# Two networks in one kernel on one core: the modulation's sums on VectorE are tied to the weight chunks, and spread at other rates

## The chip, the cores and the metric

One core of one Trainium2 chip runs one program. The metric is the device time of an execution in microseconds (us); a smaller one is better.

## What is computed

A block of a first network, with a state-space branch, a gated delta rule, a convolved gated feed-forward layer and norms, feeds a block of a second one. All tensors are float32, with 256 tokens and 2048 features. What the change touches is the second block's modulation: one vector `c` times a wide matrix, whose six parts shift, scale and gate what is around them.

```python
mod = jax.nn.silu(c) @ ada_w + ada_b
mod_c = jax.nn.silu(c_ctx) @ ada_w + ada_b
sh1, sc1, g1, sh2, sc2, g2 = jnp.split(mod[:, None, :], 6, axis=-1)
...
z = modulate(rmsnorm_2(x, norm1_g), sh1, sc1) @ w_in
zc = modulate(rmsnorm_2(xc, norm1_g), sh1c, sc1c) @ w_in
...
x = x + g1 * (jnp.concatenate([attn, rw], axis=-1) @ w_out)
x = x + g2 * swiglu(modulate(rmsnorm_2(x, norm2_g), sh2, sc2), ffn_w1, ffn_w3, ffn_w2)
```

Here `x` is the output of the first block, and `xc` is a context of 256 tokens that depends on no first block. So the columns of the context (`zc @ w_in`, and the recurrence over it) can run beside the first block's feed-forward layer.

## The kernel before

**Dense products.** Every large product is a call of `dense`. It walks through its weights in chunks of 128 x 2 x 512 floats (512 KB). `wchunk` loads a chunk into a tile `w` (three buffers, issued on SP's queue), ScalarE rounds it to a tile `wr` (L268, two buffers), and VectorE subtracts the rounded part from the chunk and leaves the rest in `wl` (L269, two buffers). TensorE then runs 24 matmuls of 256 columns on a full chunk: 16 with `wr` (L297 and L298), 8 with `wl` (L300), into accumulators `acc`, of which there are three. After the last chunk of a product ScalarE and VectorE empty the accumulators.

**The modulation.** Its first third (`ada_cols`) is a chain of matmuls and ends near 690 us. The rest is done by VectorE in `ada_rows`: a tile `w_ada` of 128 x 512 floats (256 KB) of the transposed matrix is loaded (L183, SP's queue, three buffers, two loads ahead), and one instruction (L241, called a sum below) multiplies it with a broadcast row of `c` (`ada_c`) and adds up along the row. There are 192 sums for columns 32 to 79 of `mod` and 64 for columns 80 to 95. `ada_rows` is a generator; `dense` adds `tick_rate` per chunk and runs one step of it for each whole tick, so that the rate says how many sums are traced for each chunk.

**The order.** The program is traced as the code is written, and a scheduler that goes by priorities and a simulated timeline then writes the order of each engine's queue. Each engine runs its queue in that order. The sums stand in a block of lowered priority (`high_priority(offset=-300)`): the scheduler puts them wherever it believes VectorE to have nothing better to do.

**The program's stages**, with the times at which they run in the profile of before: the last product of the first block's mixer (`w_out1`), the norm of the context, its columns (`ctx_path`) and the first slices of the feed-forward layer with the context's first recurrences, 840 to 1290 us; three more of these recurrences (`ctx_quads`) among slices of the feed-forward layer, 1290 to 1560 us; the feed-forward layer alone (`ffn1`), 1560 to 2040 us; the norms between the blocks and the columns of `x` (`rw_x`, `attn_cols`), 2040 to 2350 us; mostly attention, 2350 to 2580 us; the last recurrences, the output norms `rw_out`, the products `w_out2` and a norm, 2580 to 2780 us; the last feed-forward layer (`ffn2`), 2780 to 3520 us. Results of the 192 sums are first used after attention (`w_out2`), those of the 64 in the last products of `ffn2`.

Of the kernel before, what the change touches and what calls it, by code (L numbers as in the profile page):

```python
# [10 lines left out]
F32 = mybir.dt.float32  # L11
# [3 lines left out]
ALU = mybir.AluOpType  # L15
# [74 lines left out]
class Kern:  # L90
# [130 lines left out]
    def ada_rows(self, n0, n1):  # L221

        nc = self.nc
        W = self.a["ada_wT"].rearrange("(n p) k -> p n k", p=128)
        steps = [(q, n) for q in range(4) for n in range(n0, n1)]
        load = lambda q, n: self.ada_tile(W[:, n - 32, q * 512:q * 512 + 512])

        ahead = [load(*st) for st in steps[:2]]
        for i, (q, n) in enumerate(steps):
            if n == n0:  # L230
                ps = self.ps.tile([128, 512], F32, tag="ada", name="ada_c", bufs=1)
                for j in range(4):
                    k = q * 4 + j
                    nc.tensor.matmul(ps[:, j * 128:j * 128 + 128], lhsT=self.sil[:, k:k + 1].to_broadcast([128, 128]),
                                     rhs=self.C("ident"), start=j == 0, stop=j == 3)
            if i + 2 < len(steps):
                ahead.append(load(*steps[i + 2]))
            w = ahead.pop(0)

            with self.tc.high_priority(offset=-300):  # L240
                nc.vector.scalar_tensor_tensor(w, w, 1.0, ps, ALU.mult, ALU.mult,  # L241
                                               accum_out=self.part[:, n - n0, q:q + 1])
            yield n
        m = self.mod[:, 0, n0:n1]
        nc.vector.reduce_sum(m, self.part[:, :n1 - n0], axis=mybir.AxisListType.X)
        nc.vector.tensor_tensor(m, m, self.P("ada_b")[:, n0:n1], ALU.add)
# [15 lines left out]
    def wchunk(self, src, kb, w):  # L262
        nc = self.nc
        t = self.pw.tile([128, 2, 512], F32, tag="w", name="w", bufs=self.NW)
        nc.sync.dma_start(t[:, :kb, :w], src)
        r = self.pw.tile([128, 2, 512], F32R, tag="wr", name="wr", bufs=self.NWR)
        l = self.pw.tile([128, 2, 512], F32R, tag="wl", name="wl", bufs=self.NWL)
        nc.scalar.copy(r[:, :kb, :w], t[:, :kb, :w])  # L268
        nc.vector.tensor_tensor(l[:, :kb, :w], t[:, :kb, :w], r[:, :kb, :w].bitcast(F32), ALU.subtract)  # L269
        return r, l  # L270

    def dense(self, W, KT, c0, w, xh, xl, evac, r0=0):
# [1511 lines left out]
    def program(self, out):  # L1784
        self.setup()
        self.norm1()
        self.ada_start()
        self.qkv()
        self.deltanet()
        self.z_gate()  # L1790
        self.u_proj()
        self.dn_out()
        self.s5_setup()
        self.s5()
        self.dn_proj()
        self.gs_gate()
        self.s5_out()
        self.glu()
        self.w_out1()
        self.ada_next()  # L1800
        self.tick_rate = 0.54
        self.mod1()
        self.rw_setup()
        self.ctx_path()
        self.ffn1_norm()
        self.ctx_quads()
        self.ffn1()
        self.mid_norms()
        self.rw_x(0)
        self.run(self.rw_xq(0))  # L1810
        self.rw_x(1)
        self.attn_cols()
        self.ada_end()
        self.attention()
        self.early([self.rw_xq(1, ()), self.rw_xq(2, ('AR',)), self.rw_xq(3, ('AR',))])
        self.attn_split()
        self.x3_load()
        self.w_out2(0)
        self.rw_out_gate()
        for hq in range(4):  # L1820
            self.rw_out(hq)
        self.w_out2(1)
        self.ada_last()
        self.ffn2()
        self.final(out)
# [105 lines left out]
```

## Time and profile before

| | |
|---|---|
| median of three runs | 3553.86 us (3543.9 to 3554.04) |
| the profiled execution, its own time | 3542.68 us |
| its span, first to last instruction | 3540.7 us |
| TensorE busy | 3367.7 us (95%) |
| VectorE busy | 2431.7 us (69%) |
| ScalarE busy | 1511.8 us (43%) |
| bytes moved by DMA | 601.60 MB, mean 170 GB/s |
| mean granted TensorE clock | 0.974 |

Busy time of an engine is the time in which at least one of its instructions ran. TensorE's matmuls overlap and their ends are modelled, so that a busy TensorE is not always at its best rate. The granted clock is the share of TensorE's full clock that the chip let through, 1.00 or 0.50 at any moment. What lies outside the span is 2 us.

### The profile page before, as it was taken

To read this page: it belongs to the slowest core of one execution; us is meant where nothing else is said; L and a number is where in the kernel's file an instruction comes from. 1 tells how busy PE (TensorE), PEld (TensorE's weight loads), DVE (VectorE), ACT (ScalarE), POOL (GpSimd) and SP (SyncE) were. 2 spreads that over 40 slices of the span, in tenths; PEclk is the share of its full clock that TensorE was granted. 3 is DMA by queue.
4 is the path that set the end of the run, shared out by engine and by line. 5 is a ranking of instruction groups with operands and counts; after the bars stand their busy time and mean duration, and the time that the engine had idled before them with its cause. 6 is when DMAs were issued, how large, how long until landed. Compare 5 with 4: busy or idle time off the path is not lost. (4 is left out here: it accounts for less than half of the span.)

```text
span 3540.7 us, 72779 instructions
## 1 busy us (share of the span) xinstructions
PE 3367.7 (95%) x30748; PEld 3076.5 (87%) x30748; DVE 2431.7 (69%) x3987; ACT 1511.8 (43%) x2147; POOL 17.1 (0%) x46
## 2 busy tenths in 40 slices
PE   8999999999998899999999998997898999999998
PEld 6779877898988789899999988885686999999998
DVE  5676787867779778866665677586668655555556
ACT  4434433444344444444444454444433443433433
POOL 0000000000000000000000000000000000000000
PEclk9999999999998999999999999998899999999999
DMA  6644555557887543345555554350045555555554
GB/s 222 195 149 138 171 172 194 169 180 265 285 277 232 182 158 125 124 138 179 178 181 183 175 155 127 115 153 3 33 144 199 167 183 184 183 184 182 182 185 149
DMA packets 328071, 601.60 MB, mean 170 GB/s; under 512 B 24160, under 2 KB 48480, under 8 KB 327744
## 3 DMA queue, kind: packets, MB, share of 16 engines
q1 hardware_dynamic: 327520, 595.88, 52.2%
q8 instruction: 241, 3.95, 0.4%
q0 software_dynamic: 224, 1.07, 0.1%
q14 instruction: 86, 0.70, 0.1%
HBM read 591.61 MB, written 4.72 MB: 168 GB/s over the span
## 5 line engine op out<-in xcount | busy, mean ns | idle before, releaser
L269 DVE TENSOR_TENSOR wl<-w,wr 128x1024 fp32r<-128x1024 f32 (+2 forms) x928 | 1109.3, 1197 | 718.0 <-ACT wr L268 669.9
L268 ACT CAST wr<-w 128x1024 fp32r<-128x1024 f32 (+2 forms) x928 | 953.1, 1028 | 1416.2 <-PE acc L298 1153.1
L297 PE MATMUL acc<-hh,wr 128*128 128x256 f32 (+2 forms) x4976 | 1256.9, 288 | 29.2 <-ACT hh L1053 5.4
L298 PE MATMUL acc<-hl,wr 128*128 128x256 f32 (+2 forms) x4976 | 1248.1, 286 | 1.1 <-DVE hl L316 0.6
L297 PEld LDWEIGHTS acc<-hh,wr 128*128 128x128 f32 (+2 forms) x4976 | 958.9, 193 | 74.2 <-issue 24.8
L298 PEld LDWEIGHTS acc<-hl,wr 128*128 128x128 f32 (+2 forms) x4976 | 960.0, 193 | 14.7 <-issue 11.7
L300 PE MATMUL acc<-hh,wl 128*128 128x256 f32 (+2 forms) x4976 | 754.7, 288 | 24.1 <-DVE wl L269 23.7
L300 PEld LDWEIGHTS acc<-hh,wl 128*128 128x128 f32 (+2 forms) x4976 | 661.7, 193 | 69.9 <-DVE wl L269 35.9
L297 PE MATMUL acc<-hid,wr 128*128 128x256 f32 x1408 | 355.2, 286 | 3.7 <-DVE x L1127 3.4
L298 PE MATMUL acc<-hid,wr 128*128 128x256 f32 x1408 | 353.6, 284 | 0.0
L297 PEld LDWEIGHTS acc<-hid,wr 128*128 128x128 f32 x1408 | 271.1, 193 | 7.7 <-DVE x L1127 4.1
L298 PEld LDWEIGHTS acc<-hid,wr 128*128 128x128 f32 x1408 | 271.3, 193 | 0.9 <-issue 0.7
L300 PE MATMUL acc<-hid,wl 128*128 128x256 f32 x1408 | 224.8, 286 | 0.8 <-DVE wl L269 0.8
L241 DVE SCALAR_TENSOR_TENSOR w_ada<-w_ada,ada_c 128x512 f32<-128x512 f32 x256 | 170.1, 681 | 61.6 <-DMA w_ada<-in_ada_wT_dram 58.8
L300 PEld LDWEIGHTS acc<-hid,wl 128*128 128x128 f32 x1408 | 192.5, 192 | 4.0 <-issue 2.1
L1106 DVE SCALAR_TENSOR_TENSOR fconv<-acc,pv,fconv 128x255 f32<-128x255 f32 (+1 forms) x176 | 81.3, 477 | 23.1 <-ACT fconv L1104 21.5
L200 PE MATMUL ada_ps<-w_ada,pv 128*32 128x512 f32 x256 | 84.6, 604 | 4.4 <-DMA w_ada<-in_ada_w_dram 4.4
L1104 ACT ACTIVATE fconv<-acc,pv 128x256 f32<-128x256 f32 x88 | 40.4, 471 | 60.2 <-DVE fconv L1106 32.8
L1351 PE MATMUL rw_ps<-rw_AR,rw_BK 64*128 64x64 f32 (+1 forms) x512 | 62.4, 294 | 3.8 <-ACT rw_BKT L1358 3.6
L297 PE MATMUL acc<-mrgh,wr 128*128 128x256 f32 x256 | 63.7, 286 | 1.6 <-DVE x L1034 0.9
L1351 PEld LDWEIGHTS rw_ps<-rw_AR,rw_BK 64*128 64x128 f32 x512 | 53.8, 198 | 11.7 <-ACT rw_BKT L1358 3.8
L298 PE MATMUL acc<-ys5l,wr 128*128 128x256 f32 x256 | 63.6, 283 | 0.0
(538 smaller groups left out, 3727.0 us busy)
## 6 DMA issues: line engine op xcount, KB each, us to landing
w<-in_w_dram SPq DMA_DIRECT2D x264, 512.0 KB, 3.6
w<-in_w_in_dram SPq DMA_DIRECT2D x256, 512.0 KB, 3.9
w<-in_ffn_up_dram SPq DMA_DIRECT2D x176, 512.0 KB, 3.7
w_ada<-in_ada_wT_dram SPq DMA_DIRECT2D x256, 256.0 KB, 4.0
w<-in_ffn_down_dram SPq DMA_DIRECT2D x88, 512.0 KB, 3.6
w_ada<-in_ada_w_dram SPq DMA_DIRECT2D x128, 256.0 KB, 3.4
w<-in_w_out_dram SPq DMA_DIRECT2D x64, 512.0 KB, 4.6
w<-in_glu_w_dram SPq DMA_DIRECT2D x32, 512.0 KB, 3.6
```

The costliest lines, as they stand in the source:

```text
L200: nc.tensor.matmul(ps[32 * g:32 * g + 32, :], lhsT=self.pv[:, o + kt:o + kt + 32], rhs=ahead.pop(0), start=kt == 0, stop=kt == 15)
L241: nc.vector.scalar_tensor_tensor(w, w, 1.0, ps, ALU.mult, ALU.mult, accum_out=self.part[:, n - n0, q:q + 1])
L268: nc.scalar.copy(r[:, :kb, :w], t[:, :kb, :w])
L269: nc.vector.tensor_tensor(l[:, :kb, :w], t[:, :kb, :w], r[:, :kb, :w].bitcast(F32), ALU.subtract)
L297: nc.tensor.matmul(o, lhsT=a, rhs=xh(kt), start=kt == 0 and first_j, stop=False)
L298: nc.tensor.matmul(o, lhsT=a, rhs=xl(kt), start=False, stop=False)
L300: nc.tensor.matmul(o, lhsT=a, rhs=xh(kt), start=False, stop=kt == KT - 1 and last_j)
L1104: nc.scalar.activation(t[:, j], ps[:, j], AF.Copy, scale=w(2))
L1106: v.scalar_tensor_tensor(t[:, j, k:], ps[:, j, :256 - k], w(2 - k), t[:, j, k:], ALU.mult, ALU.add)
L1351: nc.tensor.matmul(pss[e][:, c], lhsT=bk(d, c)[hs[e]], rhs=AR[hs[e], d, :, cs], start=True, stop=True)
```

## The change

`wchunk` keeps the subtraction that it traced last as `self.wsub`. Each sum is traced in a block that puts it behind that subtraction in VectorE's queue; no wait on a semaphore is added. The rate, 0.54 sums for each chunk from `mod1` to `attn_cols` before, is 0.2 up to `ffn1_norm`, 0.55 through `ctx_quads` and `ffn1`, and 0.43 after that. `ffn2` keeps its 0.5.

```diff
-            with self.tc.high_priority(offset=-300):
+            with self.tc.high_priority(offset=-300), self.tc.issue_after(self.wsub.ins):
                 nc.vector.scalar_tensor_tensor(w, w, 1.0, ps, ALU.mult, ALU.mult,
                                                accum_out=self.part[:, n - n0, q:q + 1])
...
         nc.scalar.copy(r[:, :kb, :w], t[:, :kb, :w])
-        nc.vector.tensor_tensor(l[:, :kb, :w], t[:, :kb, :w], r[:, :kb, :w].bitcast(F32), ALU.subtract)
+        self.wsub = nc.vector.tensor_tensor(l[:, :kb, :w], t[:, :kb, :w], r[:, :kb, :w].bitcast(F32), ALU.subtract)
...
         self.ada_next()
-        self.tick_rate = 0.54
+        self.tick_rate = 0.2
         self.mod1()
         self.rw_setup()
         self.ctx_path()
         self.ffn1_norm()
+        self.tick_rate = 0.55
         self.ctx_quads()
         self.ffn1()
+        self.tick_rate = 0.43
         self.mid_norms()
```

The scheduler writes other orders from this. The first place is VectorE's queue at the end of an early slice of the first feed-forward layer, near 1190 us in the profile of before. `fconv` is the convolved output of a slice, `invDT` belongs to the recurrence over the context. Before:

```order
L241 SCALAR_TENSOR_TENSOR w_ada,part<-w_ada,ada_c 128x512 x2
L1119 TENSOR_TENSOR fconv<-fconv 128x512
L241 SCALAR_TENSOR_TENSOR w_ada,part<-w_ada,ada_c 128x512 x6
L269 TENSOR_TENSOR wl<-w,wr 128x1024
L241 SCALAR_TENSOR_TENSOR w_ada,part<-w_ada,ada_c 128x512 x2
L636 SCALAR_TENSOR_TENSOR invDT<-inv_11663,cst,invDT 128x16x16
```

And now:

```order
L1106 SCALAR_TENSOR_TENSOR fconv<-acc_13913,pv,fconv 128x254
L1119 TENSOR_TENSOR fconv<-fconv 128x512
L269 TENSOR_TENSOR wl<-w,wr 128x1024
L636 SCALAR_TENSOR_TENSOR invDT<-inv_11615,cst,invDT 128x16x16
L269 TENSOR_TENSOR wl<-w,wr 128x1024
L241 SCALAR_TENSOR_TENSOR w_ada,part<-w_ada,ada_c 128x512
L637 STREAM_TRANSPOSE invD<-invDT 128x512
```

Eight sums stood just ahead of one subtraction and two behind it; now none stands ahead of it, and a single one behind the next.

The second place is VectorE's queue in `rw_out`, near 2690 us. `xr` is an output of the recurrence, `rw_nsq` its norm. Before:

```order
L1565 SCALAR_TENSOR_TENSOR xr_25136<-rw_mean,xr_25136 128x256 x2
L241 SCALAR_TENSOR_TENSOR w_ada,part<-w_ada,ada_c 128x512 x2
L1565 SCALAR_TENSOR_TENSOR xr_25136<-rw_mean,xr_25136 128x256
L241 SCALAR_TENSOR_TENSOR w_ada,part<-w_ada,ada_c 128x512
L416 RECIPROCAL rw_nsq<-rw_nsq 64x256
L241 SCALAR_TENSOR_TENSOR w_ada,part<-w_ada,ada_c 128x512
L416 RECIPROCAL rw_nsq<-rw_nsq 64x256
L241 SCALAR_TENSOR_TENSOR w_ada,part<-w_ada,ada_c 128x512 x2
L1575 SCALAR_TENSOR_TENSOR xr_25136<-xr_25136,pv,rw_rs 128x256 x2
```

And now:

```order
L1565 SCALAR_TENSOR_TENSOR xr_25085<-rw_mean,xr_25085 128x256 x2
L416 RECIPROCAL rw_nsq<-rw_nsq 64x256 x2
L1575 SCALAR_TENSOR_TENSOR xr_25085<-xr_25085,pv,rw_rs 128x256 x2
L1576 SCALAR_TENSOR_TENSOR xr_25085<-xr_25085,pv,xv_24818 128x256 x2
L1577 TENSOR_TENSOR xr_25085<-xr_25085,rw_G_29704 128x256 x2
L316 TENSOR_TENSOR rwl_29732<-xr_25085,rwh_29730 128x256 x2
```

All 64 sums of the last part stood in this stretch; it now has four, none of them between these steps.

The third place is VectorE's queue in `ffn1` alone, near 1665 us. `hid` is the hidden layer's rounded rest. Before:

```order
L269 TENSOR_TENSOR wl<-w,wr 128x1024
L1106 SCALAR_TENSOR_TENSOR fconv<-acc_18076,pv,fconv 128x255
L1106 SCALAR_TENSOR_TENSOR fconv<-acc_18075,pv,fconv 128x255
L1106 SCALAR_TENSOR_TENSOR fconv<-acc_18076,pv,fconv 128x254
L1106 SCALAR_TENSOR_TENSOR fconv<-acc_18075,pv,fconv 128x254
```

And now:

```order
L269 TENSOR_TENSOR wl<-w,wr 128x1024
L241 SCALAR_TENSOR_TENSOR w_ada,part<-w_ada,ada_c 128x512
L1106 SCALAR_TENSOR_TENSOR fconv<-acc_18031,pv,fconv 128x255
L1106 SCALAR_TENSOR_TENSOR fconv<-acc_18030,pv,fconv 128x255
L1106 SCALAR_TENSOR_TENSOR fconv<-acc_18031,pv,fconv 128x254
L1106 SCALAR_TENSOR_TENSOR fconv<-acc_18030,pv,fconv 128x254
```

A sum now stands behind about every second subtraction of the layer, here ahead of four instructions that empty accumulators; before, the layer alone had none.

By the chunk behind which they stand, with the times that the chunks have in the profile of before, the 256 sums lie as follows:

| stretch, us | sums before | sums now |
|---|---|---|
| to 840 | 6 | 0 |
| 840 to 1290 | 186 | 32 |
| 1290 to 1560 | 0 | 34 |
| 1560 to 2040 | 0 | 88 |
| 2040 to 2350 | 0 | 36 |
| 2350 to 2580 | 0 | 2 |
| 2580 to 2780 | 64 | 4 |
| 2780 to 3520 | 0 | 60 |

The loads of `w_ada` move on SP's queue with the sums: before, up to 15 of them follow each other there; now each stands alone among the loads of `w`. TensorE's and ScalarE's queues hold the same work with small shifts of place.

## Rows read from the trace of the kernel before

**Rows 1.** The page: busy time of the engines; then the two VectorE groups.

```profile
PE 3367.7 (95%) x30748; PEld 3076.5 (87%) x30748; DVE 2431.7 (69%) x3987; ACT 1511.8 (43%) x2147; POOL 17.1 (0%) x46
...
L269 DVE TENSOR_TENSOR wl<-w,wr 128x1024 fp32r<-128x1024 f32 (+2 forms) x928 | 1109.3, 1197 | 718.0 <-ACT wr L268 669.9
...
L241 DVE SCALAR_TENSOR_TENSOR w_ada<-w_ada,ada_c 128x512 f32<-128x512 f32 x256 | 170.1, 681 | 61.6 <-DMA w_ada<-in_ada_wT_dram 58.8
```

**Rows 2.** Span and mean granted clock of the core.

```profile
core 0: 3540.7 us, clock 0.974
```

**Rows 3.** Busy time by stretch, granted clock, DMA share and rate.

```profile
core 0: us, PE busy (x) PEld busy (x) DVE busy (x) ACT busy (x) POOL busy (x), PEclk, DMA share, GB/s
840.00:1290.00 450.00, 405.14 (x3479) 379.47 (x3478) 383.60 (x800) 187.62 (x283) 4.02 (x10) 0.93 0.73 239
1290.00:1560.00 270.00, 264.14 (x3523) 244.10 (x3522) 204.68 (x341) 125.58 (x203) 3.23 (x8) 0.99 0.38 124
1560.00:2040.00 480.00, 474.75 (x3986) 468.72 (x3984) 301.42 (x371) 208.49 (x251) 1.05 (x2) 1.00 0.54 177
2040.00:2350.00 310.00, 290.35 (x2802) 266.62 (x2802) 229.62 (x405) 143.16 (x234) 1.93 (x6) 0.97 0.45 136
2350.00:2580.00 230.00, 192.62 (x2504) 149.16 (x2502) 154.22 (x330) 98.07 (x224) 4.00 (x10) 0.88 0.14 43
2580.00:2780.00 200.00, 171.19 (x1761) 146.42 (x1761) 150.25 (x321) 73.04 (x122) 0.00 (x0) 0.92 0.53 175
2780.00:3520.00 740.00, 740.00 (x6166) 738.37 (x6166) 411.88 (x422) 301.73 (x321) 0.00 (x0) 1.00 0.56 181
```

**Rows 4.** The same for the sums (L241) alone; two records for each sum.

```profile
840.00:1290.00 450.00, 124.94 (x372) 0.93 0.73 239
...
2580.00:2780.00 200.00, 42.97 (x128) 0.92 0.53 175
```

**Rows 5.** TensorE's waits, 840 to 1290 us: total us, times, longest.

```profile
PE acc L300 <- DVE wl L269: 23.9, 15, 6.5
PE rw_ps L1351 <- ACT rw_BKT L1358: 3.6, 1, 3.6
PE acc L297 <- DVE cv L1218: 3.5, 1, 3.5
```

**Rows 6.** VectorE's longest wait, 840 to 1290 us.

```profile
DVE w_ada L241 <- DMA w_ada<-in_ada_wT_dram: 41.1, 41, 2.5
```

**Rows 7.** Timeline near 1190 us: start, us, instruction, idle time before it.

```profile
1187.27 0.69 DVE L241 SCALAR_TENSOR_TENSOR w_ada<-w_ada,ada_c 128x512 f32<-128x512 f32 x1 [1.69 <-DMA w_ada<-in_ada_wT_dram]
...
1190.74 0.69 DVE L241 SCALAR_TENSOR_TENSOR w_ada<-w_ada,ada_c 128x512 f32<-128x512 f32 x1 [1.19 <-DMA w_ada<-in_ada_wT_dram]
...
1191.36 1.22 DVE L269 TENSOR_TENSOR wl<-w,wr 128x1024 fp32r<-128x1024 f32 x1
...
1192.63 1.65 PE L300 MATMUL acc<-hh,wl 128*128 128x256 f32 x6 [6.49 <-DVE wl L269]
```

**Rows 8.** The chain that ended last, 2580 to 2780 us, by line.

```profile
by line: DMA w_ada<-in_ada_wT_dram 22.9%; DVE w_ada L241 11.4%; PE acc L298 10.9%; PE acc L297 10.7%; PE acc L300 9.3%; DVE wl L269 4.6%; issue 3.1%; PE rw_pg L1547 2.5%; PE rw_pg L1546 2.3%; DVE rw_nsq L416 1.7%; DVE xr L1575 1.6%; DVE x L
```

**Rows 9.** VectorE's longest wait, 2580 to 2780 us.

```profile
DVE w_ada L241 <- DMA w_ada<-in_ada_wT_dram: 17.7, 14, 4.1
```

**Rows 10.** TensorE's longest wait, 2580 to 2780 us.

```profile
PE inv L641 <- DVE invD L637: 6.6, 1, 6.6
```

**Rows 11.** VectorE's subtractions, 1560 to 2040 us, and what ended the idle time before them.

```profile
L269 DVE TENSOR_TENSOR wl<-w,wr 128x1024 fp32r<-128x1024 f32 x161 | 196.4, 1223 | 155.2 <-ACT wr L268 153.9 <-PE acc L300 0.7
```

**Rows 12.** Timeline in `ffn1`.

```profile
1700.11 1.05 ACT L268 CAST wr<-w 128x1024 fp32r<-128x1024 f32 x1 [2.79 <-PE acc L298]
...
1701.19 1.22 DVE L269 TENSOR_TENSOR wl<-w,wr 128x1024 fp32r<-128x1024 f32 x1 [1.53 <-ACT wr L268]
```

**Rows 13.** Loads of `w_ada`, from issue to landing.

```profile
DMA to landing us min/median/max: 2.6/3.8/10.2
```

## The prediction

> **What bounds the kernel now.** I read the page first. TensorE is busy for 95% of the span, VectorE for 69%, and the sums, 256 of them, cost VectorE 170.1 us with 61.6 us of idle time before them, nearly all of it waiting for their own loads [rows 1]. A share over the whole span doesn't say whether any of that matters, so the next view is the table by stretch [rows 3]. There the reader should compare TensorE's busy time with the length of the stretch, and look at the clock. In the last feed-forward layer TensorE is busy for 740.00 of 740 us at clock 1.00, in the first one alone for 474.75 of 480: nothing that is taken off VectorE there can gain anything. Three stretches lose time: 840 to 1290, 2350 to 2580 (attention), and 2580 to 2780 us. The same table for the sums alone shows that they all lie in the first and the last of these three (but for six sums ahead of 840 us): 124.94 us of VectorE and 42.97 us [rows 4].
>
> Two losses add up in such a stretch: idle time of TensorE, and time at the half clock, in which half of the time is lost, so that a granted clock of 0.93 loses 7% of the stretch. From 840 to 1290 us that is 450 - 405.1 = 44.9 us idle and 0.07 x 450 = 31.5 us by the clock, 76 us. From 2580 to 2780 us it is 28.8 + 0.08 x 200 = 16, 45 us.
>
> Then who is late. In the first stretch TensorE's longest wait is for the subtraction L269, 23.9 us in 15 waits [rows 5], while VectorE itself waited 41.1 us in front of sums whose load had not landed [rows 6]. The timeline shows one such case whole: sums wait 1.69 and 1.19 us for loads, the subtraction behind them starts at 1191.36 at last, and TensorE, which had been out of work for 6.49 us, goes on at 1192.63 [rows 7]. In the second stretch the chain that ended last runs through the loads of the sums (22.9%) and the sums (11.4%) [rows 8], 34.3% of 200 = 68.6 us; VectorE waits 17.7 us for these loads [rows 9], and TensorE's longest wait, 6.6 us, is for a step of the recurrence that stands behind sums in VectorE's queue [rows 10]. So VectorE's queue order is what ends the waits in both, and the sums, which nobody needs there, stand in it in rows.
>
> **What the change takes out.** By the table in the section on the change, 186 sums become 32 in the first stretch and 64 become 4 in the second. A sum takes 124.94/186 = 0.67 us of VectorE [rows 4].
>
> First stretch: 154 sums x 0.67 = 103 us, and the 41.1 us of waits with them, 144 us off VectorE. How much of it reaches TensorE has a ceiling of the 76 us lost, and a floor from stretches of the same kind without a single sum. The columns of `x`, 2040 to 2350, lose 310 - 290.4 = 19.7 us idle and 0.03 x 310 = 9.3 by the clock, 29 us on 281 us of work, 10.3%. The recurrences among the feed-forward slices, 1290 to 1560, lose 5.9 + 2.7 = 8.6 us on 261, 3.3% [rows 3]. The first stretch has both kinds of work, 450 - 76 = 374 us of it; at 3.3% it would keep a loss of 12 us, at 10.3% of 39. The gain is therefore 37 to 64 us, and I take the middle, **51**, since half of its chunks are of either kind.
>
> Second stretch: 60 sums x 0.67 = 40 us, and the 17.7 us of waits, 58 us off VectorE, all of it on the chain as it stood. The other losses stay (the chain of the output norms goes through ScalarE and TensorE too). Work is 200 - 45 = 155 us; at the loss of the columns of `x` it would keep 16 us and gain 29; at that of attention, 37.4 + 0.12 x 230 = 65 us lost on 165 [rows 3], it would gain nothing; the chain's ceiling is 58. I take **35**, nearer to the 29, because the chain names sums here and not what attention waits for, and somewhat over it, since small matmuls that wait for each other count as busy and can close up too.
>
> **What it gives back.** Nothing is computed anew. The sums go to four stretches that had none: 34 (23 us of VectorE) to 1290 to 1560, 88 (59 us) to the feed-forward layer, 36 (24 us) to the columns of `x`, 60 (40 us) to the last layer. VectorE's share of these becomes (204.7 + 23)/270 = 84%, (301.4 + 59)/480 = 75%, (229.6 + 24)/310 = 82% and (411.9 + 40)/740 = 61% [rows 3]. What covers a sum in the feed-forward layer: VectorE has 155.2 us of idle time just before its subtractions there, 153.9 of it until ScalarE's `wr` is ready [rows 11], and ScalarE waits for TensorE to let go of a `wr` buffer [rows 12]. From that release at 1700.11 to the end of the subtraction at 1702.41 it is 2.3 us; TensorE meanwhile has 8 matmuls left of the released chunk, 24 of the next, and 16 of this chunk before it needs `wl`: 48, at 740/6166 = 0.12 us each [rows 3], 5.8 us. So a subtraction can come 3.5 us late, the length of five sums, and in the new order a sum stands alone.
>
> The loads: a buffer of `w_ada` is free again after its sum, and its next sum comes three sums later, 3/0.55 chunks of 24 x 0.12 us, 15.7 us; a load lands 3.8 us after issue, 10.2 at worst [rows 13]. They wait in SP's queue among the loads of `w`, which go out up to three chunks ahead of their subtraction, so a load of `w_ada` that is held up behind a `w` is still early. The 88 loads of 256 KB add 23 MB to 480 us, 48 GB/s on 177, less than the 239 GB/s at which the first stretch ran [rows 3]. The 41.1 and 17.7 us of waits go and don't come back elsewhere.
>
> If the cover is gone, the price is bounded by what the first stretch paid: 76 us lost for 125 + 41 = 166 us of sums and their waits, 0.46 us for each us on VectorE. At that price the two stretches with VectorE over 80% would pay 0.46 x (23 + 24) = 22 us, the other two 0.46 x 99 = 46. Below nothing isn't possible for added work. I take half for the two, 11 us, and 2 for the feed-forward layers, **13**.
>
> Of clock and queue the Trainium skill says two things. Its page "TensorE: Matmul & The Clock Gate" (part 1, "What's actually happening") says that for modelling the ramp costs under 1% of a typical kernel's span. Here the mean granted clock is 0.974 [rows 2], 2.6% of the span or 92 us, and 47 of these lie in the two stretches; by the rule all would be at most 35 us, the share of the two 18, and the gain, scaled with the loss (121 to 92 us), 65 in place of 86: 3491 us. The measurement decides here, and I keep 86.
>
> **The sum.** 51 + 35 - 13 = 73 us. The profiled execution took 3542.7 us by its own time, so 3470 us. The median of the three runs lies 11 us above that execution, though one run agrees with it; I put the forecast in the middle, **3475 us**.
>
> **Rivals.** (a) The stretches stay slow without the sums, since hand-offs between engines set them: then the floors hold, 37 and some 15 us, less 20 given back in the denser stretches: 32, 3511 us. For it speaks that the columns of `x` lose 10% with no sum in them; against it that the longest waits name the subtraction, with sums ahead of it. (b) All of it comes off the chain and nothing is given back: 64 + 58 = 122, 3421 to 3426 us. Against it speaks that VectorE gets over 80% busy in two stretches.
>
> (c) Slower: a sum behind a subtraction stands ahead of the instructions that empty the accumulators, and where TensorE is at 100% each sum holds it up. 218 sums go to such stretches; with 86 us gained it turns into a loss from 0.39 us for each, and at the whole 0.67 us it costs 146: 3603 us. The skill says on the same page (part 1, "Architectural detail", on queue depths) that VectorE's queue is strictly first in, first out; the trace agrees [rows 7]. Against (c) stand the 3.5 us of room above and the 61 to 75% of VectorE in the two large stretches, which hold 148 of the 218.
>
> (d) The scheduler bunches the sums again, and the change does nothing: 3554 us. The new order shows the opposite.
>
> **How the numbers follow.** Likeliest case, 3445 to 3495 us: 0.65. (a), to 3530: 0.18. (b), under 3445: 0.10. (c): 0.04. (d) and no change for other reasons: 0.03. The range 3438 to 3520 us takes in most of (a) and the nearer edge of (b). 0.3% (11 us) is what a measurement of this kernel can tell from no change; all of the first three cases lie beyond it. Faster 0.93, same 0.03, slower 0.04.
>
> **What would show it.** Right: from 840 to about 1240 us TensorE's wait for L269 falls well under 10 us and the clock goes to 0.97 or more; VectorE's waits for loads of `w_ada` fall from 59 us to a few; the stretch of `rw_out` gets about 35 us shorter; the feed-forward layers keep their length within 2 us. Wrong: new waits of TensorE for L269 or for emptied accumulators in the feed-forward layers or the columns of `x`; waits of sums for their loads as large as before; or a first stretch whose waits now name L1218, ScalarE or the recurrence with the same total.

## The result, and the profile after

The changed kernel takes 3492.48 us (median of four runs, 3483.39 to 3493.35), the kernel before 3552.78 us beside it; the ratio is 0.984, with a 95% interval of 0.9824 to 0.9855. The profiled execution took 3492.46 us, 50.2 us less than that of before. Beside the experiments one execution of merged (3625.83 us, mean clock 0.836) and one of the kernel before (5286.49 us, 0.553) ran in a slower state, and all medians and ratios below leave them out.

The page first, with the lines that answer to [rows 1]: busy time of the engines, then the two VectorE groups.

```profile
PE 3360.2 (96%) x30748; PEld 3070.3 (88%) x30748; DVE 2428.0 (70%) x3987; ACT 1513.5 (43%) x2147; POOL 17.0 (0%) x46
...
L269 DVE TENSOR_TENSOR wl<-w,wr 128x1024 fp32r<-128x1024 f32 (+2 forms) x928 | 1111.0, 1198 | 749.2 <-ACT wr L268 684.5
...
L241 DVE SCALAR_TENSOR_TENSOR w_ada<-w_ada,ada_c 128x512 f32<-128x512 f32 x256 | 173.9, 680 | 1.6 <-PE ada_c L234 1.0
```

The busy times of the engines are those of before within 0.3%. What fell is the idle time in front of the sums, from 61.6 us to 1.6, and no load of theirs is named any more.

For a table of where the time went, each trace is cut at the same work and not at the same time: where the 193rd, 321st, 385th, 529th, 625th, 641st and 673rd subtraction L269 starts. These are the rows of the changed kernel (length of the stretch, busy time of each engine, granted clock, DMA share, GB/s), from the program's start to its end.

```profile
0.00:790.04 790.04, 774.00 (x6069) 633.74 (x6070) 552.95 (x928) 342.78 (x459) 2.89 (x10) 0.99 0.55 175
790.04:1239.06 449.02, 433.29 (x3900) 408.24 (x3900) 321.62 (x526) 218.61 (x336) 4.02 (x10) 0.98 0.55 177
1239.06:1517.03 277.97, 272.61 (x3562) 252.89 (x3557) 228.62 (x416) 126.14 (x197) 3.09 (x8) 0.98 0.48 157
1517.03:1949.56 432.53, 423.76 (x3550) 420.15 (x3549) 313.74 (x486) 184.10 (x218) 0.00 (x0) 1.00 0.68 223
1949.56:2307.27 357.71, 335.48 (x3175) 310.70 (x3174) 278.46 (x521) 161.06 (x256) 2.98 (x8) 0.97 0.54 169
2307.27:2561.85 254.58, 220.74 (x2649) 173.01 (x2648) 176.19 (x376) 107.72 (x237) 4.00 (x10) 0.85 0.17 54
2561.85:2728.61 166.76, 151.58 (x1638) 127.38 (x1637) 101.07 (x173) 68.77 (x119) 0.00 (x0) 0.94 0.33 109
2728.61:3490.69 762.08, 748.68 (x6225) 744.17 (x6223) 455.36 (x565) 304.32 (x327) 0.00 (x0) 0.99 0.62 198
```

These are four rows of the kernel before, cut in the same way: the context, `ffn1`, the norms and the last layer.

```profile
785.44:1289.51 504.07, 457.94 (x3900) 428.00 (x3899) 416.65 (x852) 215.09 (x328) 4.02 (x10) 0.94 0.73 240
...
1568.52:1992.47 423.95, 419.51 (x3506) 416.23 (x3505) 264.54 (x324) 183.88 (x217) 0.00 (x0) 1.00 0.55 178
...
2594.42:2781.58 187.16, 158.35 (x1653) 133.58 (x1653) 136.21 (x290) 67.86 (x116) 0.00 (x0) 0.92 0.53 175
2781.58:3540.71 759.13, 746.07 (x6201) 741.57 (x6199) 421.71 (x443) 304.41 (x327) 0.00 (x0) 0.99 0.56 179
```

The next table has the lengths of these stretches in us for all kernels of this study, one profiled execution of each, cut in the same way. "Chunks" are the subtractions; "context" is `w_out1`'s end, the context's columns and the first slices, "norms" the stretch with `rw_out`.

| kernel | start, to 192 | context, to 320 | quads, to 384 | ffn1, to 528 | columns of x, to 624 | attention, to 640 | norms, to 672 | ffn2, to the end | span |
|---|---|---|---|---|---|---|---|---|---|
| before | 785.4 | 504.1 | 279.0 | 424.0 | 353.1 | 248.8 | 187.2 | 759.1 | 3540.7 |
| changed | 790.0 | 449.0 | 278.0 | 432.5 | 357.7 | 254.6 | 166.8 | 762.1 | 3490.7 |
| changed, once more | 785.9 | 449.9 | 279.5 | 432.5 | 357.2 | 255.4 | 166.1 | 762.1 | 3488.6 |
| rates_only | 785.5 | 507.8 | 280.6 | 424.0 | 351.8 | 249.6 | 188.4 | 759.1 | 3546.7 |
| pin_only | 788.3 | 449.5 | 279.9 | 433.2 | 357.8 | 247.0 | 167.2 | 762.1 | 3484.9 |
| last_free | 785.3 | 452.2 | 276.9 | 432.5 | 355.7 | 256.9 | 183.3 | 759.2 | 3501.9 |
| no_sums | 786.0 | 439.8 | 276.4 | 424.0 | 352.4 | 257.2 | 173.3 | 759.2 | 3468.3 |
| thin_sums | 787.1 | 446.2 | 275.0 | 427.4 | 352.7 | 253.0 | 170.1 | 762.1 | 3473.7 |
| before_thin | 786.8 | 485.9 | 276.1 | 423.9 | 350.4 | 253.2 | 182.1 | 759.2 | 3517.5 |
| before_no_loads | 788.6 | 476.8 | 275.6 | 421.3 | 350.9 | 252.8 | 184.4 | 759.2 | 3509.6 |
| merged | 785.4 | 453.2 | 285.7 | 432.0 | 354.4 | 248.3 | 164.6 | 762.2 | 3485.7 |
| spread | 791.5 | 446.5 | 277.5 | 430.7 | 354.5 | 247.9 | 163.3 | 761.7 | 3473.5 |

The context's stretch gained 55 us, that of the norms 20. The feed-forward layer lost 8.5, the columns of `x` 4.6, the last layer 3.0. The start and attention, which the change hardly touches, were 4.6 and 5.8 us longer in this execution. Together 50.

In the context's stretch the wait for the subtraction, 23.9 us in [rows 5], is gone. These are TensorE's longest waits from 790 to 1239 us of the changed kernel.

```profile
PE acc L298 <- DVE hl L316: 3.1, 2, 2.1
PE rw_pt L1357 <- DVE rw_N L1354: 2.8, 2, 2.1
PE rw_ps L1351 <- ACT rw_BKT L1358: 2.2, 1, 2.2
PE acc L297 <- ACT wr L268: 2.2, 3, 1.3
PE acc L300 <- DVE wl L269: 1.5, 2, 0.8
```

In the stretch of the norms neither a sum nor a load of one is among the costly lines of the chain that ended last, where they were 34.3% of it [rows 8].

```profile
by line: PE acc L297 20.1%; PE acc L298 19.9%; PE acc L300 19.1%; PE ss L329 3.2%; DVE rw_nsq L416 3.2%; PE rw_pg L1547 3.0%; PE rw_pg L1546 2.9%; PE ns L405 2.3%; issue 2.0%; PE rw_rs L424 1.9%; PE rw_mean L1564 1.9%; PE rw_p L1415 1.3%; P
```

What TensorE still waits for from 2540 to 2728 us are the steps of the norms themselves.

```profile
PE rw_rs L424 <- DVE rw_nsq L416: 4.4, 3, 2.0
PE ns L405 <- ACT sq L1567: 3.8, 5, 1.0
PE acc L297 <- ACT hh L1053: 3.5, 1, 3.5
```

### The profile page after: what moved, and what is told of

It is laid out like the page before. It is cut to its first block, busy times and chain, and to the rows that moved or that the text cites. A ratio compares the mean times of both kernels' runs of the same rounds, so it can differ in the third digit from the quotient of the medians.

```text
span 3490.7 us, 72546 instructions
## 1 busy us (share of the span) xinstructions
PE 3360.2 (96%) x30748; PEld 3070.3 (88%) x30748; DVE 2428.0 (70%) x3987; ACT 1513.5 (43%) x2147; POOL 17.0 (0%) x46
## 4 chain that ended last, share of the span: by engine, by line
PE 88%; DVE 8%; ACT 2%; issue 1%; DMA 1%; SPq 0%; ACTq 0%; DVEq 0%; POOLq 0%
PE acc L297 25%; PE acc L300 24%; PE acc L298 24%; PE ada_ps L200 2%; DVE wl L269 2%; PE rw_ps L1351 1%; PE s_py L959 1%; PE s_pw L939 1%; PE ss L329 1%; ACT wr L268 1%; PE rw_pS L1451 1%; PE rw_p L1415 1%; PE at_ps L1666 1%; PE at_pt L1682 1%; PE at_po L1688 1%
## 5 line engine op out<-in xcount | busy, mean ns | idle before, releaser
L269 DVE TENSOR_TENSOR wl<-w,wr 128x1024 fp32r<-128x1024 f32 (+2 forms) x928 | 1111.0, 1198 | 749.2 <-ACT wr L268 684.5
L241 DVE SCALAR_TENSOR_TENSOR w_ada<-w_ada,ada_c 128x512 f32<-128x512 f32 x256 | 173.9, 680 | 1.6 <-PE ada_c L234 1.0
L1106 DVE SCALAR_TENSOR_TENSOR fconv<-acc,pv,fconv 128x255 f32<-128x255 f32 (+1 forms) x176 | 81.3, 476 | 13.6 <-ACT fconv L1104 11.9
L1104 ACT ACTIVATE fconv<-acc,pv 128x256 f32<-128x256 f32 x88 | 40.5, 471 | 53.7 <-DVE fconv L1106 31.3
L297 PE MATMUL acc<-ys5h,wr 128*128 128x256 f32 x256 | 63.4, 283 | 0.0
L298 PE MATMUL acc<-mrgl,wr 128*128 128x256 f32 x256 | 63.1, 283 | 0.0
```

The costliest lines, as they stand in the source:

```text
L269: self.wsub = nc.vector.tensor_tensor(l[:, :kb, :w], t[:, :kb, :w], r[:, :kb, :w].bitcast(F32), ALU.subtract)
L297: nc.tensor.matmul(o, lhsT=a, rhs=xh(kt), start=kt == 0 and first_j, stop=False)
L298: nc.tensor.matmul(o, lhsT=a, rhs=xl(kt), start=False, stop=False)
L1104: nc.scalar.activation(t[:, j], ps[:, j], AF.Copy, scale=w(2))
L1106: v.scalar_tensor_tensor(t[:, j, k:], ps[:, j, :256 - k], w(2 - k), t[:, j, k:], ALU.mult, ALU.add)
```

## The experiments

Theory: the sums cost time where they stand in rows, ahead of a subtraction and ahead of their own loads. Tying each to a subtraction takes the rows apart; how many stand in the context's columns is of no account. The chief rival is the other half of the change: the rates, which keep sums out of the context's columns.

**The sums tied, the rates as before (pin_only).**

```diff
         self.ada_next()
-        self.tick_rate = 0.2
+        self.tick_rate = 0.54
...
-        self.tick_rate = 0.55
...
-        self.tick_rate = 0.43
```

> The sums are tied to the subtractions, but the rate stays 0.54 from the context's columns to attention; 48 sums instead of 32 stand in the stretch that was 840 to 1290 us before, none less in the last one. Theory 1 (what counts is that no sum stands in a row ahead of a subtraction or ahead of its own load): most of the gain stays, at 0.46 us of TensorE for each us of VectorE the 16 more sums cost 16 x 0.67 x 0.46 = 5 us: 3497 us. Theory 2 (the number of sums in the context's columns decides, the rates do the work): the first stretch gives back a good part of its 55 us, 3515 us or more.

Measured: 3479.68 us, ratio 0.9799 (0.9782 to 0.9816). The context's stretch:

```profile
788.30:1237.75 449.45, 437.88 (x3908) 413.33 (x3908) 331.25 (x558) 218.46 (x336) 4.02 (x10) 0.97 0.59 186
```

449.45 us with 48 sums against 449.02 and 449.89 with 32 in the two executions of the changed kernel: the 16 more cost nothing that can be seen, and the 5 us that the theory charged for them are not there. Tying alone has the whole gain. Whether the old rate is even better than the new ones isn't settled: the total lies below the changed kernel's, but the stretch that differs is attention. There the changed kernel has three sums and pin_only none; merged has three too and is as short there (248.3 us), so the sums are not the difference.

**The rates alone (rates_only).**

```diff
-            with self.tc.high_priority(offset=-300), self.tc.issue_after(self.wsub.ins):
+            with self.tc.high_priority(offset=-300):
```

> The three rates are changed, but the sums are not tied to the subtractions. In the written order the sums lie as before: 186 in the context's stretch, 64 in that of the output norms. Theory 1: the time of before, 3553 us, within 0.3%. Theory 2 (the rates do the work): near 3500 us.

Measured: 3547.81 us beside 3548.35, ratio 1.0 (0.9989 to 1.0011). The rates, without the tie, do nothing: in the trace 192 sums still run in the context's stretch and 61 in that of the norms. The rival has fallen.

**The last 64 sums left free (last_free).**

```diff
-            with self.tc.high_priority(offset=-300), self.tc.issue_after(self.wsub.ins):
+            pin = self.tc.issue_after(self.wsub.ins) if n0 < 80 else ExitStack()
+            with self.tc.high_priority(offset=-300), pin:
```

> Only the 192 sums of the first two calls are tied; the 64 of the last call are free, and stand again in the stretch of the output norms. Theory 1 (the two stretches are independent, and the second one is worth the 20 us that its chunks gained in the two traces): 3492 + 20 - 3 (the last layer is free of them) = 3509 us, and that stretch as long as before, some 187 us for its chunks. Rival (as forecast, the second stretch is worth 35 us, and the 20 us are an accident of the clock in that execution): 3524 us.

Measured: 3506.15 us, ratio 0.9871 (0.9854 to 0.9888). The stretch of the norms and the last layer:

```profile
2559.41:2742.71 183.30, 158.50 (x1653) 134.06 (x1652) 136.58 (x291) 69.86 (x119) 0.00 (x0) 0.90 0.57 179
2742.71:3501.86 759.15, 746.07 (x6201) 741.57 (x6199) 421.83 (x443) 304.39 (x327) 0.00 (x0) 0.99 0.60 179
```

The norms are 17 us longer than in the changed kernel, and the last layer 3 us shorter. So the second stretch is worth some 17 to 20 us, and the forecast's 35 was too much. The granted clock in it lies between 0.88 and 0.96 over the kernels of the table, so a few us of such a difference can be the clock; TensorE's idle time there is 24.8 us here and 15.2 in the changed kernel.

**No sums, no loads, no broadcasts (no_sums).** Columns 32 to 95 of the modulation are left at the bias.

```diff
-        steps = [(q, n) for q in range(4) for n in range(n0, n1)]
+        steps = []
+        nc.vector.memset(self.part, 0.0)
```

> Leaves out all 256 sums, their loads, and the matmuls L234 that broadcast c; columns 32 to 95 of the modulation are the bias alone. What is left is what the placing of the sums can reach at best. Theory 1 (the new order hides the sums but for the some 16 us that the feed-forward layers, the columns of x and the clock gave back): 3474 to 3480 us, with a loss in the context's stretch and in that of the output norms that stays: 25 us of TensorE in the latter, from the hand-offs of the norms. Rival (the new order still pays for the sums in the context's stretch and in the output norms): under 3460 us, and the loss in the latter under 12 us.

Measured: 3462.74 us (3449.94 to 3474.86), ratio 0.9749 (0.9716 to 0.9782). The norms and the last layer:

```profile
2535.84:2709.14 173.30, 159.01 (x1631) 130.66 (x1630) 99.28 (x165) 68.53 (x119) 0.00 (x0) 0.88 0.31 98
2709.14:3468.30 759.16, 746.07 (x6201) 741.58 (x6199) 421.83 (x443) 304.40 (x327) 0.00 (x0) 0.99 0.60 179
```

The total is lower than the theory gave, by the 9 us that the context's stretch lost too, so that part of the expectation was wrong: 32 sums there, with their loads and broadcasts, still cost 9 us. But the norms are no shorter than in the changed kernel (173.3 against 166.8): 14.3 us of TensorE's idle time and 0.12 x 173.3 = 21 us by the clock stay with no sum in the program. By the idle time, 14.3 us against the 15.2 of the changed kernel, the change has taken out what the sums cost TensorE in the second stretch. The length alone can't tell, since the clock was lower here (0.88 against 0.94).

**Thin sums (thin_sums).** Each works on 32 of 512 columns; loads, sums and broadcasts stay, in their places.

```diff
-                nc.vector.scalar_tensor_tensor(w, w, 1.0, ps, ALU.mult, ALU.mult,
+                nc.vector.scalar_tensor_tensor(w[:, :32], w[:, :32], 1.0, ps[:, :32], ALU.mult, ALU.mult,
```

> The changed kernel, but each sum works on 32 of its 512 columns, so that the results of columns 32 to 95 are wrong; all loads, the 256 sums as instructions and the matmuls L234 that broadcast c (96 records) stay. The feed-forward layer alone (its chunks 385 to 528) took 424.0 us before, 432.5 in the changed kernel and 424.0 without sums, loads and broadcasts. Theory 1 (of these 8.5 us some 4 are TensorE's idle time behind emptied accumulators that came late on VectorE, and the other 4 are the broadcasts that moved into a stretch in which TensorE is full): 428 us there, and the last layer as long as in the changed kernel, 762.1 us, since its 3 us are broadcasts alone. Rival (the loads of w_ada hold up those of w): 432 us. Second rival (all of it is VectorE's time): 424 us, and 759 us for the last layer.

Measured: 3476.45 us, ratio 0.9805 (0.978 to 0.983). The layer `ffn1` and the last one:

```profile
1508.26:1935.69 427.43, 422.17 (x3515) 419.45 (x3514) 273.38 (x481) 183.92 (x217) 0.00 (x0) 1.00 0.71 226
...
2711.52:3473.66 762.14, 748.68 (x6225) 744.18 (x6223) 428.33 (x565) 304.39 (x327) 0.00 (x0) 0.99 0.65 198
```

Both come out as the first theory said: 427.4 and 762.1 us. Of the 8.5 us that `ffn1` lost, 5.1 go with VectorE's time and 3.4 stay; of the last layer's 3.0 all stay. (Of the 5.1, TensorE's idle time is 3.5. The other 1.6 are busy time: some small matmuls of the recurrence lie ahead of the cut in thin_sums.) What stays are the loads and the broadcasts. The loads run at the same 223 to 226 GB/s in both kernels, so they are not what the 5.1 us are. In the last layer the 3.0 us are the broadcasts and not loads that came late: from before to the changed kernel TensorE's busy time there grew by 2.6 us (746.07 to 748.68) with 24 matmuls more (6201 to 6225), its idle time by 0.3 us only. In `ffn1` the broadcasts' own time fits what stays. This is the busy time of L234 in the changed kernel, for `ffn1` with its edges, the columns of `x` and the last layer (the first number is TensorE's, with the records).

```profile
1510.00:1990.00 480.00, 3.31 (x24) 3.00 (x24) 1.00 0.68 223
1990.00:2302.00 312.00, 2.37 (x16) 2.02 (x16) 0.97 0.52 161
2728.00:3468.00 740.00, 3.79 (x24) 3.24 (x24) 1.00 0.63 202
```

**The kernel before with thin sums (before_thin).** The same edit in the kernel before.

> The kernel before, but each sum works on 32 of its 512 columns (columns 32 to 95 of the modulation come out wrong); the loads stay whole, and the sums stand where they stood: 186 in the context's stretch, 64 in that of the output norms. What is taken away is most of VectorE's own time for the sums, what stays is their waiting for loads. In the two traces the context's stretch (chunks 193 to 320) went from 504 to 449 us and that of the output norms (chunks 641 to 672) from 187 to 167. Theory 1 (the queue is held up by sums whose load hasn't landed, as much as by the sums themselves): the context's stretch comes out between, at 470 to 495 us, and the waits for loads stay at 40 us or rise. Rival (VectorE's time for the sums was the whole cost): 445 to 455 us.

Measured: 3519.28 us, ratio 0.9908 (0.9883 to 0.9933). Context and norms by stretch:

```profile
786.76:1272.64 485.88, 451.86 (x4044) 421.13 (x4045) 329.01 (x853) 219.05 (x339) 4.14 (x10) 0.97 0.75 249
...
2576.30:2758.35 182.05, 160.02 (x1659) 134.67 (x1659) 108.05 (x290) 68.71 (x119) 0.00 (x0) 0.91 0.56 180
```

VectorE's wait for loads from 840 to 1290 us:

```profile
DVE w_ada L241 <- DMA w_ada<-in_ada_wT_dram: 80.1, 80, 3.9
```

With sums of about a quarter of the time (184 ns), the waits for loads double from 41.1 [rows 6] to 80.1 us, and only 18 of the 55 us come back.

**The kernel before without the loads (before_no_loads).** The sums read a constant tile.

```diff
-        load = lambda q, n: self.ada_tile(W[:, n - 32, q * 512:q * 512 + 512])
+        load = lambda q, n: self.pw.tile([128, 512], F32, tag="wa", name="w_ada", bufs=3)
...
-                nc.vector.scalar_tensor_tensor(w, w, 1.0, ps, ALU.mult, ALU.mult,
+                nc.vector.scalar_tensor_tensor(w, self.cst[:, :512], 1.0, ps, ALU.mult, ALU.mult,
```

> The kernel before, but without the 256 loads of w_ada: each sum reads a constant tile in place of its load (columns 32 to 95 come out wrong) and takes its whole time on VectorE; 170 sums stand in the context's stretch, 22 ahead of it, 64 in that of the output norms. What is taken away is the waiting for loads and 67 MB of traffic. Theory 1 (sums in a row delay the subtraction by themselves too): the context's stretch stays well over the 449 us of the changed kernel, at 465 to 490 us, and that of the output norms over 172 us. Rival (the waiting for loads was the whole cost): 450 to 455 and 167 us.

Measured: 3509.35 us, ratio 0.9881 (0.9857 to 0.9905).

```profile
788.57:1265.40 476.83, 442.75 (x3991) 416.24 (x3991) 413.17 (x852) 218.33 (x338) 4.03 (x10) 0.97 0.47 149
...
2565.99:2750.40 184.41, 160.93 (x1643) 134.80 (x1642) 134.32 (x288) 68.80 (x118) 0.00 (x0) 0.88 0.28 90
```

Here 27 of the 55 us come back. Both halves of the cost are real. In the stretch of the norms either alone keeps most of the 20 us, 15 and 18 of them (182 and 184 us long, against 187 before and 167 in the changed kernel). These are rough, since the clock was 0.91 and 0.88 there.

**One walk instead of two (merged), so that c is broadcast 8 times and not 12.** `mod` became one row of 128 columns to make room.

```diff
-        self.ada = itertools.chain(self.ada_rows(32, 64), self.ada_rows(64, 80))
+        self.ada = self.ada_rows(32, 80)
```

> The changed kernel with one walk over columns 32 to 79 instead of two over 32 to 63 and 64 to 79, so that c is broadcast 8 times and not 12: 64 records of L234 and not 96, in the same stretches. Theory 1 (a broadcast costs TensorE its own time, some 0.14 us for each record, wherever TensorE is full): 32 fewer are 4 us over the stretches from 1240 to 2310 us; in the total that is about what a median can tell, 3488 us beside the 3492 of the changed kernel. Rival (broadcasts are hidden): no stretch shorter.

Measured: 3479.99 us (median of three, 3478.8 to 3487.47), ratio 0.9813 (0.9793 to 0.9832), beside 3486.12 (3485.69 to 3490.38) for the changed kernel on the same chip: not to be told apart. `ffn1` has 16 records instead of 24 and is 0.5 us shorter, the columns of `x` none instead of 16 and 3 us shorter; the quads were 6 us longer, at a clock of 0.96 against 0.98. The three stretches together, in which the theory looked for 4 us, are 1072 us long against 1068 and 1069 in the two executions of the changed kernel: inconclusive.

**Sums begun earlier, and away from emptied accumulators (spread).** The merged kernel, with

```diff
-    tick_rate = 0.33
+    tick_rate = 0.37
...
-        self.glu()
-        self.w_out1()
         self.ada_next()
-        self.tick_rate = 0.2
+        self.tick_rate = 0.5
+        self.glu()
+        self.w_out1()
+        self.tick_rate = 0.05
...
-        self.tick_rate = 0.55
+        self.tick_rate = 0.62
...
-        self.tick_rate = 0.43
+        self.tick_rate = 0.12
...
-            while self.ticks >= 1:
+            if self.ticks >= 1 and (KT < 16 or 4 <= k0 < KT - 2):
```

> The merged walk, begun before the products of the gated unit (glu) instead of after w_out1, at rates 0.5 (glu, w_out1), 0.05 (context's columns), 0.62 (ctx_quads, ffn1), 0.12 (columns of x), at most one sum for a chunk, and none in the first two chunks and the last of a product with eight chunks, where VectorE empties accumulators. 20 sums run before 840 us, 39 in the stretch that was 840 to 1290 us, 39 and 94 in the next two, none in the columns of x. Theory 1 (what is left to gain is the 5 us in the columns of x, 4 of TensorE's idle time in the feed-forward layer, 4 of broadcasts): 10 to 13 us under the changed kernel, 3480 us. Rival (a sum in any place costs the same 0.1 us): no gain beyond the 4 us of the broadcasts.

Measured: 3476.41 us (3471.34 to 3479.24), ratio 0.9795 (0.9777 to 0.9814).

```profile
1515.44:1946.16 430.72, 423.11 (x3545) 419.23 (x3542) 318.45 (x503) 183.98 (x218) 0.00 (x0) 1.00 0.72 230
1946.16:2300.66 354.50, 335.86 (x3158) 310.63 (x3156) 260.37 (x450) 160.44 (x257) 2.98 (x8) 0.97 0.47 141
```

The first of these rates is that of the modulation's first third, which so ends earlier. spread has the lowest median of the whole computation here, 10 us under the changed kernel on the same chip, with no run of the one within the range of the other; from pin_only, whose runs go from 3475.17 to 3486.65, it can't be told. The two profiled executions differ by 15 us: 2.7 in the columns of `x` and 1.8 in `ffn1`, as the theory has it; 7.5 in attention, where merged is as short without this edit, so that this part isn't shown to be its doing; 8 in the context, the quads and the norms; and the start, which got 20 sums, is 5.6 longer.

**The changed kernel once more (after_again).**

> The changed kernel once more, beside the others on one chip. Theory 1 (the 1% by which executions of one kernel differ is the clock in stretches that the change doesn't touch): the stretches of the feed-forward layers within 1 us of the first profile, 432.5 and 762.1 us; the start and attention differ by up to 10 us together with their time at the half clock. Rival (the stretches themselves differ): 3 us or more in the feed-forward layers too.

Measured: 3486.12 us, ratio 0.9827 (0.9811 to 0.9842). The start and `ffn1` of this execution:

```profile
0.00:785.90 785.90, 768.77 (x6069) 629.86 (x6070) 552.86 (x928) 342.84 (x459) 2.89 (x10) 1.00 0.58 176
...
1515.33:1947.80 432.47, 423.70 (x3550) 420.09 (x3549) 313.77 (x486) 184.09 (x218) 0.00 (x0) 1.00 0.71 223
```

The feed-forward layers repeat to 0.1 us, so the 8.5 and 3.0 us are the change's own. The start is 4.1 us shorter than in the first profile of the same program, at clock 1.00 and not 0.99: that part of the first difference is chance. Attention is as long as in the first profile (255.4 and 254.6 us), and in rates_only as long as in the kernel before (249.6 and 248.8), which speaks for the order and against chance. But it varies from 247 to 257 us over the kernels, and is 257 without any sum, so whether the new order has a part in the 6 us stays open.

## Why the prediction was right, and where it was not

The forecast was 3475 us, in 3438 to 3520, faster; it came to 3492, faster. The sum had 73 us for the profiled execution, and 50 were measured: the norms gave 15 less, the start and attention, which the sum left out, took 10, 2 more were given back, and the context gave 4 more. By its steps:

**What bounds the kernel: right.** VectorE's queue order ended the waits in the two stretches. rates_only and pin_only show that the tie, and not the rates, made the difference, before_thin and before_no_loads that a row of sums holds the queue by its own time and by its loads, each for a part.

**The context's stretch, 51 us: right,** 55 measured. TensorE's wait for L269 fell from 23.9 to 1.5 us, the clock went from 0.94 to 0.98 by these chunks. The assumed price of the sums that stay was too high by pin_only, where 16 more cost nothing, though no_sums shows that 32 of them still cost 9 us against none.

**The stretch of the norms, 35 us: the term that was mis-sized; it is 20** (17 by last_free). The working let 16 of the 45 us lost there stay, by the columns of `x`, which gives 29, and went above that toward the chain's 58; but 58 is more than the 45 us that were lost, so it was no ceiling. What stays is 15.2 us of idle time and 0.06 x 166.8 = 10 us by the clock, 25 us, and no_sums keeps 35, with as much idle time. Rival (a), with 15 us for this stretch, came nearer to the 20: the hand-offs of the norms, `rw_nsq`, `sq` and `hh`, are what TensorE still waits for once the sums are gone. The addition for small matmuls that "can close up too" had no row behind it; TensorE's busy time there did fall, by 6.8 us (158.35 to 151.58), but the broadcasts that left the stretch were 5.65 us of it.

**What it gives back, 13 us: right in sum, wrong in its parts.** Measured are 8.5 in `ffn1`, 3.0 in the last layer, 4.6 in the columns of `x` and -1.0 among the quads, 15 us. The forecast had 11 for the denser two, which gave 3.6, and 2 for the layers, which gave 11.5; that the two errors nearly cancel is luck. Its sign that the layers keep their length within 2 us failed. The step that failed is the list of what moves: a moved sum takes with it the matmuls that broadcast `c`, which lay in stretches in which TensorE idled, and now stand in layers in which it is full. They are 3 us in each layer. The other 5 in `ffn1` go with VectorE's time. The margin of 3.5 us for a subtraction held (no wait for L269 there); what the margin left out were the emptied accumulators behind a sum. These are all of TensorE's waits in `ffn1` before, 1568 to 1993 us:

```profile
PE acc L297 <- ACT fconv L1104: 4.2, 6, 0.7
```

And in the changed kernel, 1517 to 1950 us:

```profile
PE acc L297 <- ACT fconv L1104: 6.0, 6, 1.3
PE acc L297 <- DVE x L1127: 1.6, 2, 0.8
PE acc L297 <- DVE fconv L1106: 1.1, 2, 0.7
```

They grew by 4.5 us, and none names a load. The longest shows how: a sum runs ahead of VectorE's part in emptying the accumulators (L1106), ScalarE's next part (L1104) waits for that, and TensorE for ScalarE.

```profile
1691.83 0.68 DVE L241 SCALAR_TENSOR_TENSOR w_ada<-w_ada,ada_c 128x512 f32<-128x512 f32 x1
...
1692.43 1.65 DVE L1106 SCALAR_TENSOR_TENSOR fconv<-acc,pv,fconv 128x255 f32<-128x255 f32 x4
...
1693.72 0.47 ACT L1104 ACTIVATE fconv<-acc,pv 128x256 f32<-128x256 f32 x1 [2.33 <-DVE fconv L1106]
...
1694.23 0.36 PE L297 MATMUL acc<-hh,wr 128*128 128x256 f32 x1 [1.31 <-ACT fconv L1104]
```

**Loads and waits: right.** Of the 1.6 us that VectorE still sat idle before the sums, 1.0 is a wait for a broadcast, so less than 1 us can be waits for loads.

**The rule on the clock.** The Trainium skill, "TensorE: Matmul & The Clock Gate" (part 1, "What's actually happening"), puts the cost of the clock's ramp at under 1% of a typical kernel's span. The prediction took that as a bound on all time at the half clock, which that page of the skill doesn't say; the mean clock of 0.975 in the changed kernel is 2.5%. So taken it would have put the gain of the two stretches at 65 us in place of 86; they gained 75. So the 3491 us of that reading, though close to the time, isn't how it came about: the clock term was counted rightly in the context's stretch (0.94 to 0.98), and too high in that of the norms, where it went from 0.92 to 0.94 only.

**Rivals.** (b) did not happen, and (d) is what rates_only is. (c) did not happen as a whole, but it shows in the columns of `x`, where TensorE waits longer for the subtraction. Its wait (total, count and longest, in us) in the kernel before, from 1992 to 2346 us:

```profile
PE acc L300 <- DVE wl L269: 5.6, 6, 1.4
```

and in the changed kernel, from 1949 to 2307 us:

```profile
PE acc L300 <- DVE wl L269: 9.1, 5, 3.3
```

These are 3.5 us more, in a stretch that lost 4.6. In thin_sums, from 1936 to 2288 us, where the same 16 records of L234 stand:

```profile
PE acc L300 <- DVE wl L269: 4.9, 3, 3.3
```

There the stretch takes 352.7 us, as long as in no_sums (352.4), which speaks for VectorE's time for the sums. But merged, which keeps that time and takes away the 16 records, is 3 us shorter there too, and other waits changed as well. So how the 4.6 us divide stays open.

## What to carry to other kernels

Work that nobody waits for should be tied to a steady beat of the queue in which it stands, and its loads with it: here a low priority alone let the scheduler drop it in rows, and such a row delayed the step behind it by its own time and by its loads. When a step is moved, count all that it issues on every engine: 24 matmuls that broadcast `c` cost 3 us in the last layer, where TensorE is full. That such matmuls are free where TensorE has idle time is likely but not shown: in the columns of `x` thin_sums speaks for it and merged against it. And when a wait is taken away, look for the next hand-off in that stretch before the whole loss is booked as gain.

## What was not expected of the hardware

- One program, two executions, the same instructions: the start of the changed kernel took 790.04 us at a mean clock of 0.99 and 785.90 us at 1.00. The clock also fell to half (1.2 GHz) while TensorE was busy all the time. In the windows of the first execution:

```profile
386.10:392.90 6.80, 6.80 (x28) 5.70 (x27) 6.13 (x14) 1.35 (x2) 0.00 (x0) 0.50 0.25 77
```

In those of the second, from the same place in the work:

```profile
384.80:391.60 6.80, 6.80 (x47) 5.71 (x45) 6.80 (x16) 2.24 (x3) 0.00 (x0) 1.00 0.34 91
```

TensorE is busy throughout in both, and 28 matmuls ran at 0.50 where 47 ran at 1.00. The first execution stood 386.10 - 384.80 = 1.3 us behind at the beginning of this stretch. At its end the same matmuls start at these times in the first and in the second:

```profile
392.59 1.28 PE L939 MATMUL s_pw<-s_u,s_b 32*128 32x256 f32 x4
```

```profile
388.60 1.12 PE L939 MATMUL s_pw<-s_u,s_b 32*128 32x256 f32 x4
```

It is 4.0 us behind there, so 2.7 of the start's 4.1 us came in this one fall. Such a fall can make part of the 0.3% by which runs of one kernel differ here; what sets it off stays open.

- The sum takes 680 ns on 512 columns (681 in [rows 1]) and 181 ns on 32, as this group of thin_sums has it (the second number after the bar is the mean in ns), so (680 - 181)/480 = 1.04 ns for each column more.

```profile
L241 DVE SCALAR_TENSOR_TENSOR w_ada<-w_ada,ada_c 128x32 f32<-128x32 f32 x256 | 46.0, 181 | 1.5 <-PE ada_c L234 0.7 <-DMA w<-in_w_dram 0.3
```

The page "VectorE: DVE Perf Modes" of the Trainium skill gives VectorE a clock of 0.96 GHz (section Specifications) and one result per cycle in its base mode (section "Mode 1× (REGULAR) — the baseline"). That is 1/0.96 = 1.04 ns for each column; the trace agrees, with 1.04 ns.
